# Moving the weight-split subtractions at the phase meetings from GpSimd to VectorE in a three-block transformer kernel

## The chip, the cores and the metric

One core of a Trainium2 chip runs the whole program. The metric is the device time of one execution in microseconds; a time is the median of several runs. The engines are named as the profile names them: PE is TensorE's matmuls and PEld its weight loads, DVE is VectorE, ACT is ScalarE, POOL is GpSimd, SP is SyncE, which issues most of the DMAs.

## What is computed

Three blocks follow each other on one sequence of 512 tokens, 1024 features wide, in float32. The first is gated linear attention and an MLP, the second stick-breaking attention and an MLP, the third a block that mixes an mLSTM with latent attention, and an MLP again. The reference, cut to the parts that carry the weights:

```python
def sq_relu_mlp(x, w_up, w_down):
    h = jax.nn.relu(x @ w_up)
    return (h * h) @ w_down
...
for layer in range(DEPTH):                       # two layers
    mix = gla_mixer(...) if layer < N_A else ... @ sb_w_o[j]
    h = layer_norm(DEEPNORM_ALPHA * h + mix, ln_g[layer, 0], ln_b[layer, 0])
    h = layer_norm(DEEPNORM_ALPHA * h + sq_relu_mlp(h, mlp_w_up[layer], mlp_w_down[layer]),
                   ln_g[layer, 1], ln_b[layer, 1])
...
x = x + jnp.concatenate([y_a, y_b], axis=-1) @ w_out[l]
h = rms_norm(x, g_ffn_norm[l])
x = x + jnp.square(jax.nn.relu(h @ w_ff1[l])) @ w_ff2[l]
```

## The kernel before

Activations lie feature-major: 128 partitions, eight chunks of features, 512 tokens. Every float32 matmul is done as three matmuls in the fp32r format, on a high and a low half of each operand (`mm3`, L273): the high half is the value cast to fp32r, the low half is what the cast lost. `H` and `L` are the two halves of the activations between phases, `ah` and `al` those of the hidden layer of an MLP or of an attention's output, `wh` and `wl` those of a weight tile.

Weights come as a stream of tiles of 1024 x 256 (`run`, from L1666: the list `order`). Each tile is fetched by SP in two pieces `raw`, each 128 x 1024 elements, four such buffers in all. `_split` (L196) makes the two halves of each piece: ScalarE casts `raw` to `wh` (L222), and another engine subtracts, `wl = raw - wh` (L224). A tile has two pieces, so four instructions. `q` counts quarters of a tile: the first piece is `q` 0 and 1, the second `q` 2 and 3. Tiles of the `up` matrices in the middle of an MLP go another way (`_combine`, L229), always on VectorE.

The phases meet in `boundary` (L589). It runs the last jobs of one phase (an output or down projection) on the two halves of the tokens, A and B, one after the other; behind each half the norm over it is started, in steps that are let in between the matmuls of the next jobs; then the first jobs of the next phase run on A and on B. A norm goes: residual sums into `Z` (L450, or L688), sums over pairs of chunks into `acc` (L458), their `fold` (L462), a matmul `st` with a constant matrix that spreads the mean (L473), subtraction of the mean (L516), squares `pt` on ScalarE (L478), again `acc`, `fold` and `st`, scaling (L523), gain and bias (L527), and the split into `H` (ScalarE, L503) and `L` (L505; the first two pairs of chunks on GpSimd, the last two on VectorE). `z_from_h` (L438) then forms `Z` from `H + L` (L444), half of it on GpSimd. The norm before the third block also scales `Z` on GpSimd (L548).

The order of PE's instructions is written by hand there (`manual_schedule`, L592). The orders of VectorE, ScalarE, GpSimd and SP are made by a scheduler at build time; each engine then works through its own queue strictly in that order. GpSimd's queue also holds some small DMAs (`small_load`, L142), among them the weights `wuq` and `wuk` of the latent attention.

Where `eased` (L1684) names the tile's range in the stream, the subtraction for the second piece of the tile goes to GpSimd (L223). There are five ranges, around the meetings: output projection and first `up` tiles in either layer, last `down` tiles and what follows them, and output projection and first tiles of the last MLP.

Of the kernel before, what the change touches and what calls it, by code (L numbers as in the profile page):

```python
# [10 lines left out]
F32 = mybir.dt.float32  # L11
# [3 lines left out]
ALU = mybir.AluOpType  # L15
# [48 lines left out]
class Weights:  # L64
# [5 lines left out]
    def at(self, k, cols):  # L70
        return tuple(x[:, k % self.nk, cols] for x in self.parts[k // self.nk])
# [21 lines left out]
class Model:  # L93
# [65 lines left out]
        return hi, lo  # L159


    def stream(self, order, fast, home, later, eased):


        self.order, self.fast, self.home, self.later, self.eased = order, fast, home, later, eased
        self.raws, self.ws, self.done = {}, {}, {}
        self.pos = 0

# [27 lines left out]
    def _split(self, i, n=4):  # L196

        if i >= len(self.order) or i < self.pos or i in self.later and len(self.slots) == 1:
            return
        if i in self.fast:  # L200
            if i not in self.ws:
                self._dma(i)
                self.ws[i], self.done[i] = {}, self._combine(i)
            for _ in range(1 if n < 4 else 3):
                next(self.done[i], None)
            return
        nc = self.nc
        if i not in self.ws:
            self._dma(i)
            self.ws[i], self.done[i] = Weights([], 4), 0  # L210
        parts, w, q = self.ws[i].parts, self.order[i][2], self.done[i]
        self.done[i] = min(4, q + n)
        while q < self.done[i]:

            g = q // 2
            if g == len(parts):
                parts.append(self.half_tile(i, g))
            hi, lo = parts[g]
            e = min(self.done[i], g * 2 + 2)
            a = slice(q % 2 * 2, q % 2 * 2 + (e - q) * 2)  # L220
            r = self.raws[i][g][:, a, :w]
            nc.scalar.copy(hi[:, a, :w], r)  # L222
            eng = nc.gpsimd if q >= 2 and any(p0 <= i < p1 for p0, p1 in self.eased) else nc.vector  # L223
            eng.tensor_tensor(lo[:, a, :w], r, hi[:, a, :w].bitcast(F32), op=ALU.subtract)  # L224
            q = e
        if q == 4:
            self.raws.pop(i, None)
# [1436 lines left out]
    def run(self):  # L1664
        nc = self.nc
        n4 = lambda n: [(n, i, 256) for i in range(4)]  # L1666
        mlp = lambda u, d: [(x, q * 4 + i, 256) for q in range(4) for x in (u, d) for i in range(4)]
        order = n4("gla_v")
        for hp in range(2):
            order += [("gla_q", hp, 256), ("gla_k", hp, 256), ("gla_g", hp * 2, 256), ("gla_g", hp * 2 + 1, 256)]  # L1670
        order += n4("gla_o") + mlp("up0", "down0") + n4("sb_v")
        order += [("sb_qk", i, 256) for i in range(8)]
        order += n4("sb_o") + mlp("up1", "down1")
        order += [("w2_q", 0, 256), ("w2_k", 0, 256), ("w2_cq", 0, 256), ("w2_ck", 0, 208)]
        order += [("w2_v", 0, 256), ("w2_o", 0, 256), ("w2_v", 1, 256), ("w2_o", 1, 256)]
        order += [("w2_out", 2, 256), ("w2_out", 3, 256)]
        order += [("w2_out", 0, 256), ("w2_out", 1, 256)] + mlp("ff1", "ff2")
        at = lambda n, i: next(j for j, o in enumerate(order) if o[:2] == (n, i))

        fast = {at(n, i) for n in ("up0", "up1", "ff1") for i in range(4, 16 if n == "ff1" else 15)}  # L1680
        home = {at(*x) for n in ("down0", "down1", "ff2") for x in ((n, 0), (n, 12))}
        home |= {at(*x) for x in (("gla_o", 0), ("sb_o", 0), ("w2_out", 0), ("sb_qk", 0), ("w2_v", 0))}

        eased = [(at(*a), at(*b) + 3) for a, b in (  # L1684
            (("gla_o", 1), ("up0", 3)), (("down0", 13), ("sb_v", 3)), (("sb_o", 1), ("up1", 3)),
            (("down1", 13), ("w2_ck", 0)), (("w2_out", 0), ("ff1", 3)))]
        later = {at(n, i) for n in ("gla_o", "sb_o") for i in (2, 3)}
        self.stream(order, fast, home, later, eased)
        self.setup()

        V, C = {}, {}
        for l in range(2):
            A, acc, acc2 = [], {}, {}
            out = self.out_jobs("gla_o" if l == 0 else "sb_o", A, acc)
            if l == 0:
                self.gla(A, out)
            else:
                self.sb(V, A, out)
                self.exp_tables()
            self.open_z()  # L1700
            self.open_edge()
            self.z_from_h()
            acc.update({0: self.new_acc(), 256: self.new_acc()})
            mlp = self.mlp_jobs(f"up{l}", f"down{l}", acc2)
            self.boundary(out, lambda seg: self.layer_norm(2 * l, acc[seg.start], seg), mlp[0][0])
            self.z_from_h()
            self.es.close()
            self.middle(mlp, self.Z, 1)
            self.open_edge()
            acc2.update({0: self.new_acc(), 256: self.new_acc()})  # L1710
            if l == 0:
                self.boundary(mlp[3][1], lambda seg: self.layer_norm(1, acc2[seg.start], seg), self.sb_v_jobs(V))
            else:
                def norm(seg):
                    yield from self.layer_norm_rms(3, acc2[seg.start], seg, C)
                self.xs = nc.dram_tensor("x_mid", (P, KC, S), F32).ap()
                self.boundary(mlp[3][1], norm, self.mix_first_jobs(C))
            self.es.close()
            self.zs.close()
        A = [None] * 8  # L1720
        out = self.out2_jobs(A)
        self.mix2(C, A, out[0])
        self.open_edge()
        mlp = self.mlp_jobs("ff1", "ff2", None, resid=False, final=self.out)

        def norm(seg):
            acc = self.new_acc()
            for p in range(4):
                self.square_sum(acc, p, self.zp(p, seg))
            yield from self.rms_norm("g_ffn", seg, acc, 1)  # L1730
        self.boundary(out, norm, mlp[0][0])
        self.es.close()
        self.middle(mlp, None, 0)
        self.run_jobs(mlp[3][1][:3])
        for seg in (A_, B_):
            mlp[3][1][3](seg)
        self.es.close()
        self.zs.close()
# [109 lines left out]
```

## Time and profile before

| | us |
|---|---|
| median of 3 runs | 1824.34 |
| lowest, highest | 1823.04, 1825.54 |
| the profiled execution | 1826.51 |
| its span, first to last instruction | 1824.6 |
| PE busy | 1765.2 |
| DVE busy | 1175.0 |
| ACT busy | 973.8 |
| POOL busy | 276.5 |

The busy times are of the profiled execution. Rows of the timeline give the start of an instruction in us from the first one, its duration in us, the engine, the line of the kernel, the operation, what it writes and reads, shapes, a count where equal rows follow each other, and in brackets how long the engine had stood before it and what ended that. The granted clock is given as a share of full speed.

### The profile page before, as it was taken

How to read it: one execution, taken by the hardware profiler on the slowest of the kernel's cores; microseconds unless marked ns; L12 is line 12 of the kernel's file. 1: busy time of each engine (PE TensorE's matmuls, PEld its weight loads, DVE VectorE, ACT ScalarE, POOL GpSimd, SP SyncE). 2: the span in 40 equal slices, each digit the busy share in tenths (PEclk: the TensorE clock that was granted, in tenths of full speed). 3: DMA queues.
4: the chain of work that ended last, by engine and by line, in shares of the span. 5: the costliest groups of instructions: out<-in, count | busy, mean ns of one | idle time of the engine just before them, and what ended most of it. 6: DMA issues, size and time to landing. Idle time of an engine off the chain costs nothing. (4 is left out here: it accounts for less than half of the span.)

```text
span 1824.6 us, 29591 instructions
## 1 busy us (share of the span) xinstructions
PE 1765.2 (97%) x11816; PEld 1606.5 (88%) x11816; DVE 1175.0 (64%) x1774; ACT 973.8 (53%) x1942; POOL 276.5 (15%) x315
## 2 busy tenths in 40 slices
PE   8999999999999999989999999988999999999999
PEld 8889998989899978878989898988887798989897
DVE  4545667656557388878567565483886867756562
ACT  5445464627264378764626354454777654545370
POOL 1001330000013233353300000153001321000000
PEclk9999999999999999999999999999999999999999
DMA  5212322324233111113224142332102222233231
GB/s 197 93 47 70 116 72 91 105 81 137 71 127 106 47 58 59 47 46 117 70 70 138 59 139 70 105 111 85 48 15 93 66 74 93 93 106 102 94 116 47
DMA packets 47626, 158.79 MB, mean 87 GB/s; under 512 B 5168, under 2 KB 8896, under 8 KB 47488
## 3 DMA queue, kind: packets, MB, share of 16 engines
q1 hardware_dynamic: 44752, 150.88, 25.5%
q0 software_dynamic: 1296, 3.92, 0.6%
q8 instruction: 93, 1.52, 0.3%
q10 hardware_dynamic: 1440, 2.10, 0.3%
q14 instruction: 45, 0.37, 0.1%
HBM read 152.68 MB, written 4.19 MB: 86 GB/s over the span
## 5 line engine op out<-in xcount | busy, mean ns | idle before, releaser
L275 PE MATMUL mm<-ah,wh 128*128 128x512 f32 (+1 forms) x1264 | 435.0, 344 | 3.5 <-DVE Z L1658 2.5
L276 PE MATMUL mm<-al,wh 128*128 128x512 f32 (+1 forms) x1264 | 431.8, 342 | 3.5 <-DVE al L669 2.1
L277 PE MATMUL mm<-ah,wl 128*128 128x512 f32 (+1 forms) x1264 | 430.6, 341 | 1.6 <-DVE wl L224 1.1
L224 DVE TENSOR_TENSOR wl<-raw,wh 128x1024 fp32r<-128x1024 f32 (+1 forms) x192 | 221.2, 1157 | 88.5 <-ACT wh L222 85.8
L222 ACT CAST wh<-raw 128x1024 fp32r<-128x1024 f32 (+2 forms) x238 | 223.1, 951 | 101.7 <-PE mm L276 65.0
L276 PEld LDWEIGHTS mm<-al,wh 128*128 128x128 f32 x1264 | 239.3, 189 | 34.3 <-DVE al L669 3.0
L275 PEld LDWEIGHTS mm<-ah,wh 128*128 128x128 f32 x1264 | 239.3, 189 | 33.9 <-DVE Z L1658 2.7
L277 PEld LDWEIGHTS mm<-ah,wl 128*128 128x128 f32 x1264 | 239.3, 189 | 30.9 <-DVE wl L224 1.5
L275 PE MATMUL mm<-H,wh 128*128 128x256 f32 (+1 forms) x704 | 228.9, 325 | 0.2 <-ACT sl L1198 0.2
L224 POOL TENSOR_TENSOR wl<-raw,wh 128x1024 fp32r<-128x1024 f32 (+2 forms) x46 | 118.7, 2588 | 723.4 <-ACT wh L222 681.2
L276 PE MATMUL mm<-L,wh 128*128 128x256 f32 (+1 forms) x704 | 219.8, 312 | 4.5 <-DVE L L505 4.5
L277 PE MATMUL mm<-H,wl 128*128 128x256 f32 (+1 forms) x704 | 219.6, 312 | 0.0
L275 PE MATMUL mm<-wh,H 128*128 128x256 f32 (+2 forms) x568 | 165.6, 292 | 6.9 <-ACT wh L222 6.9
L276 PE MATMUL mm<-wl,H 128*128 128x256 f32 (+2 forms) x568 | 160.9, 283 | 0.0
L277 PE MATMUL mm<-wh,L 128*128 128x256 f32 (+2 forms) x568 | 160.2, 282 | 0.0
L236 ACT CAST wh<-S 128x1024 fp32r<-128x1024 f32 x68 | 71.3, 1048 | 166.6 <-PE mm L276 152.0
L276 PEld LDWEIGHTS mm<-L,wh 128*128 128x128 f32 x704 | 134.9, 192 | 8.8 <-DVE L L505 5.3
L277 PEld LDWEIGHTS mm<-H,wl 128*128 128x128 f32 x704 | 134.2, 191 | 8.2
L275 PEld LDWEIGHTS mm<-H,wh 128*128 128x128 f32 x704 | 134.7, 191 | 6.6 <-issue 0.8
L237 DVE TENSOR_TENSOR wl<-S,wh 128x1024 fp32r<-128x1024 f32 x68 | 83.2, 1223 | 74.8 <-ACT wh L236 74.8
L688 DVE TENSOR_TENSOR Z<-Z,mm 128x512 f32<-128x512 f32 (+1 forms) x98 | 57.4, 587 | 102.7 <-PE mm L277 102.6
L275 PEld LDWEIGHTS mm<-wh,H 128*128 128x128 f32 x568 | 109.0, 192 | 8.8 <-ACT wh L222 7.6
(409 smaller groups left out, 3936.0 us busy)
## 6 DMA issues: line engine op xcount, KB each, us to landing
raw<-in_up SPq DMA_DIRECT2D x64, 512.0 KB, 4.0
raw<-in_down SPq DMA_DIRECT2D x64, 512.0 KB, 3.7
raw<-in_ff SPq DMA_DIRECT2D x64, 512.0 KB, 3.9
raw<-in_sb_qk SPq DMA_DIRECT2D x16, 512.0 KB, 3.6
raw<-in_gla_g SPq DMA_DIRECT2D x8, 512.0 KB, 4.2
raw<-in_gla_o SPq DMA_DIRECT2D x8, 512.0 KB, 3.7
raw<-in_sb_v SPq DMA_DIRECT2D x8, 512.0 KB, 4.2
raw<-in_sb_o SPq DMA_DIRECT2D x8, 512.0 KB, 3.5
```

Of the source, the lines that this page charges most:

```text
L222: nc.scalar.copy(hi[:, a, :w], r)
L224: eng.tensor_tensor(lo[:, a, :w], r, hi[:, a, :w].bitcast(F32), op=ALU.subtract)
L236: nc.scalar.copy(pair[0], t)
L237: tt(pair[1], t, pair[0].bitcast(F32), op=ALU.subtract)
L275: mm(ps, l[0], r[0], start=start, stop=False)
L276: mm(ps, l[0], r[1], start=False, stop=False)
L277: mm(ps, l[1], r[0], start=False, stop=stop)
L688: nc.vector.tensor_tensor(self.Z[:, c, seg], self.Z[:, c, seg], ps, op=ALU.add)
```

## The change

The list `eased` and the choice of engine are taken out. All subtractions of `_split` are issued on VectorE. 46 instructions are affected; their number of bytes, the casts before them, the tiles and the DMAs are the same.

```diff
-    def stream(self, order, fast, home, later, eased):
+    def stream(self, order, fast, home, later):
...
-        self.order, self.fast, self.home, self.later, self.eased = order, fast, home, later, eased
+        self.order, self.fast, self.home, self.later = order, fast, home, later
...
             nc.scalar.copy(hi[:, a, :w], r)
-            eng = nc.gpsimd if q >= 2 and any(p0 <= i < p1 for p0, p1 in self.eased) else nc.vector
-            eng.tensor_tensor(lo[:, a, :w], r, hi[:, a, :w].bitcast(F32), op=ALU.subtract)
+            nc.vector.tensor_tensor(lo[:, a, :w], r, hi[:, a, :w].bitcast(F32), op=ALU.subtract)
...
-        eased = [(at(*a), at(*b) + 3) for a, b in (
-            (("gla_o", 1), ("up0", 3)), (("down0", 13), ("sb_v", 3)), (("sb_o", 1), ("up1", 3)),
-            (("down1", 13), ("w2_ck", 0)), (("w2_out", 0), ("ff1", 3)))]
...
-        self.stream(order, fast, home, later, eased)
+        self.stream(order, fast, home, later)
```

Behind L223 of the kernel before, all lines of the changed kernel have a number smaller by one or more (L224 becomes L223, L505 becomes L504). The orders of PE and SP are the same in both builds. VectorE's order, from the last `L` of half A to the fold of half B, where the first output projection meets the first MLP; `wl18` and `wl19` are tiles of `up0`, and the middle number is the piece. Before:

```order
L505 TENSOR_TENSOR L_82<-pt_256_2337,H_81 128x2x256
L444 TENSOR_TENSOR Z_226_1955<-H_81,L_82 128x2x256
L224 TENSOR_TENSOR wl18_0_2414<-raw18_0_2409,wh18_0_2413 128x1024
L505 TENSOR_TENSOR L_82<-pt_257_2343,H_81 128x2x256
L450 SCALAR_TENSOR_TENSOR Z_226_1955<-Z_226_1955,mm_260_2421 128x256
L444 TENSOR_TENSOR Z_226_1955<-H_81,L_82 128x2x256
L224 TENSOR_TENSOR wl19_0_2481<-raw19_0_2476,wh19_0_2480 128x1024
L450 SCALAR_TENSOR_TENSOR Z_226_1955<-Z_226_1955,mm_261_2447 128x256
L458 TENSOR_TENSOR acc_233_1980<-acc_233_1980,Z_226_1955 128x512
L462 TENSOR_TENSOR fold_262_2474<-acc_233_1980 128x256
```

The two second pieces, `wl18_1` and `wl19_1`, are in GpSimd's queue here. The same stretch of VectorE's queue in the changed kernel:

```order
L504 TENSOR_TENSOR L_82<-pt_256_2337,H_81 128x2x256
L449 SCALAR_TENSOR_TENSOR Z_226_1955<-Z_226_1955,mm_260_2421 128x256
L443 TENSOR_TENSOR Z_226_1955<-H_81,L_82 128x2x256
L223 TENSOR_TENSOR wl18_0_2414<-raw18_0_2409,wh18_0_2413 128x1024
L504 TENSOR_TENSOR L_82<-pt_257_2343,H_81 128x2x256
L223 TENSOR_TENSOR wl18_1_2418<-raw18_1_2411,wh18_1_2417 128x1024
L449 SCALAR_TENSOR_TENSOR Z_226_1955<-Z_226_1955,mm_261_2447 128x256
L223 TENSOR_TENSOR wl19_0_2481<-raw19_0_2476,wh19_0_2480 128x1024
L457 TENSOR_TENSOR acc_233_1980<-acc_233_1980,Z_226_1955 128x512
L223 TENSOR_TENSOR wl19_1_2485<-raw19_1_2478,wh19_1_2484 128x1024
L461 TENSOR_TENSOR fold_262_2474<-acc_233_1980 128x256
```

Both second pieces now stand between the last `L` and the fold, one residual sum has moved ahead of the last `L`, and one `Z` has moved behind the fold.

GpSimd's queue ahead of the latent attention's first weights, with the semaphores that each row waits for. `KLp` is a tile of that attention that is set to zero, `wl101_1` the second piece of a weight tile of the third block. Before:

```order
L1427 MEMSET KLp_1609_13785 64x512 [waits PE_49,Pool_49]
L224 TENSOR_TENSOR wl101_1_13814<-raw101_1_13218,wh101_1_13813 128x512 [waits PE_49,DMAHW7_49,Activation_49,Pool_49]
L224 TENSOR_TENSOR wl101_1_13814<-raw101_1_13218,wh101_1_13813 128x512 [waits Activation_49]
L142 DMA wuq_1574_13651<-in_w_uq 128x384
L142 DMA wuk_1575_13653<-in_w_ukv 128x256
```

The two subtractions wait for the casts on ScalarE, and the DMAs behind them wait for nothing of their own. In the changed kernel:

```order
L1426 MEMSET KLp_1609_13785 64x512 [waits PE_49,Pool_49]
L142 DMA wuq_1574_13651<-in_w_uq 128x384 [waits PE_49]
L142 DMA wuk_1575_13653<-in_w_ukv 128x256
L142 DMA wuq_1625_13895<-in_w_uq 128x384
L142 DMA wuk_1626_13897<-in_w_ukv 128x256 [waits DMASW2_49]
```

The subtractions are gone from it, and the first DMA has a wait for PE instead.

VectorE's queue where the second MLP meets the third block, from the sums of squares of half A to the fold. `wl98` is a tile of the third block. Before:

```order
L458 TENSOR_TENSOR acc_1470_12782<-acc_1470_12782,pt_1473_12794 128x512
L224 TENSOR_TENSOR wl98_0_12871<-raw98_0_12866,wh98_0_12870 128x1024
L458 TENSOR_TENSOR acc_1470_12782<-acc_1470_12782,pt_1474_12799 128x512
L688 TENSOR_TENSOR Z_1178_8873<-Z_1178_8873,mm_1479_12904 128x256
L462 TENSOR_TENSOR fold_1475_12803<-acc_1470_12782 128x256
```

In the changed kernel:

```order
L457 TENSOR_TENSOR acc_1470_12782<-acc_1470_12782,pt_1473_12794 128x512
L687 TENSOR_TENSOR Z_1178_8873<-Z_1178_8873,mm_1479_12904 128x256
L457 TENSOR_TENSOR acc_1470_12782<-acc_1470_12782,pt_1474_12799 128x512
L223 TENSOR_TENSOR wl98_0_12871<-raw98_0_12866,wh98_0_12870 128x1024
L461 TENSOR_TENSOR fold_1475_12803<-acc_1470_12782 128x256
L223 TENSOR_TENSOR wl98_1_12875<-raw98_1_12868,wh98_1_12874 128x1024
```

The first piece's subtraction has moved behind the last `acc`, directly ahead of the fold, and the second piece's stands behind the fold. On ScalarE the square `pt_1474_12799` has moved ahead of the cast to `wh98_0_12870`; that is the only difference in ScalarE's order.

## Rows read from the trace of the kernel before

**Rows 1.** The page's part 1: busy us (share of the span) x instructions.
```profile
PE 1765.2 (97%) x11816; PEld 1606.5 (88%) x11816; DVE 1175.0 (64%) x1774; ACT 973.8 (53%) x1942; POOL 276.5 (15%) x315
```
**Rows 2.** PE's waits by releaser: us in total, times, longest us.
```profile
PE st L473 <- DVE fold L462: 9.5, 6, 4.7
...
PE mm L276 <- DVE L L505: 4.5, 2, 2.3
...
PE mm L276 <- DVE al L669: 2.1, 2, 1.1
...
PE pa L1563 <- DVE E L1551: 1.5, 3, 0.8
```
**Rows 3.** GpSimd's instructions on tile `wl`: ns min/median/max; idle before, us, times.
```profile
L224 POOL TENSOR_TENSOR wl<-raw,wh x46: 1267/2510/3390, 182.0 to 1519.6; 128x1024 fp32r<-128x1024 f32 x41, 128x512 fp32r<-128x512 f32 x4, 128x832 fp32r<-128x832 f32 x1
...
  ACT wh L222: 681.2, 32
```
**Rows 4.** DVE by line and form (busy us, mean ns), engines' busy us, both 300:530.
```profile
L224 DVE TENSOR_TENSOR wl<-raw,wh 128x1024 fp32r<-128x1024 f32 x20 | 24.5, 1225 | 11.6 <-ACT wh L222 11.0
...
300.00:530.00 230.00, 230.00 (x1472) 207.53 (x1471) 137.84 (x182) 110.74 (x176) 0.00 (x0) 1.00 0.30 98
```
**Rows 5.** Timelines of DVE, POOL and PE, first meeting, 228 to 240 us.
```profile
228.84 0.68 DVE L505 TENSOR_TENSOR L<-pt,H 128x512 fp32r<-128x512 f32 x1
...
231.30 2.85 DVE L505 TENSOR_TENSOR L<-pt,H 128x512 fp32r<-128x512 f32 x1
234.07 0.41 DVE L450 SCALAR_TENSOR_TENSOR Z<-Z,mm 128x256 f32<-128x256 f32 x1
...
238.43 0.69 DVE L458 TENSOR_TENSOR acc<-acc,Z 128x512 f32<-128x512 f32 x1
239.16 0.42 DVE L462 TENSOR_TENSOR fold<-acc 128x256 f32<-128x256 f32 x1
...
230.32 6.07 POOL L224 TENSOR_TENSOR wl<-raw,wh 128x1024 fp32r<-128x1024 f32 x2 [2.73 <-ACT wh L222]
...
234.20 0.38 PE L276 MATMUL mm<-L,wh 128*128 128x256 f32 x1 [2.33 <-DVE L L505]
239.64 0.70 PE L473 MATMUL st<-fold,onesd 128*128 128x256 f32 x2 [0.23 <-DVE fold L462]
```
**Rows 6.** Busy PE, PEld, DVE, ACT, POOL, then PEclk, in stretches of low clock.
```profile
234.57:237.97 3.40, 3.40 (x19) 3.40 (x18) 3.40 (x2) 1.22 (x3) 1.82 (x1) 0.50 0.46 157
...
1210.78:1217.59 6.81, 4.64 (x19) 4.46 (x20) 6.15 (x6) 2.06 (x6) 3.92 (x2) 0.50 0.97 333
1268.81:1275.62 6.81, 5.08 (x16) 4.76 (x17) 0.00 (x0) 0.79 (x4) 0.00 (x0) 0.50 0.25 97
```
**Rows 7.** Timelines of ACT, POOL, DVE and PE before the third block, 1207 to 1213.
```profile
1207.17 1.03 ACT L222 CAST wh<-raw 128x1024 fp32r<-128x1024 f32 x1
1208.57 0.63 ACT L478 ACTIVATE pt<-Z 128x512 f32<-128x512 f32 x1 [0.36 <-POOL Z L548]
...
1210.27 4.43 POOL L224 TENSOR_TENSOR wl<-raw,wh 128x1024 fp32r<-128x1024 f32 x2 [1.73 <-issue]
...
1210.46 2.44 DVE L462 TENSOR_TENSOR fold<-acc 128x256 f32<-128x256 f32 x1
...
1212.95 1.22 PE L473 MATMUL st<-fold,onesd 128*128 128x256 f32 x2 [4.75 <-DVE fold L462]
```
**Rows 8.** Timelines of PE, ACT, POOL at `wuq`, 1255 to 1271; tile `wuq`.
```profile
1255.05 0.26 PE L275 MATMUL mm<-wh,H 128*128 128x208 f32 x1
...
1264.55 0.73 ACT L1366 ACTIVATE cT<-pa,vec 128x512 f32<-128x512 f32 x1
...
1265.31 0.61 POOL L142 DMA_DIRECT2D wuq<-in_w_uq  x1
...
1270.54 1.62 PE L1391 MATMUL qp<-wuq,cT 128*128 128x192 f32 x4 [6.07 <-DMA wuq<-in_w_uq]
...
DMA to landing us min/median/max: 2.7/3.9/5.1
```

## Prediction

> **What bounds the kernel now.** I read the page's busy time first: TensorE works 1765.2 of 1824.6 us [rows 1]. So the time is its matmuls plus some 59 us in which it stands, and an edit off TensorE can only change that standing time and the clock that follows it. PE's instructions and their order are the same in both builds, so its work is taken as fixed. Next I read PE's waits by releaser [rows 2]: `st` on `fold`, 9.5 us in six waits (the longest 4.75, the row of 1212.95), matmuls on `L`, 4.5 in two, on `al`, 2.1 in two, on `E`, 1.5 in three. All four are released by VectorE, which is busy only 64% of the span, so the question is what delays VectorE at those moments.
>
> The timeline of the first meeting of phases answers it [rows 5]. `L` at L505 takes 0.68 us at 228.84. The next one, of the same shape, takes 2.85: it starts at 231.30 while GpSimd is in the first of two low-half subtractions (230.32, 6.07 us for both), and PE stands 2.33 us for it. At the place before the mixers the `fold` takes 2.44 us instead of the 0.42 of rows 5, again beside GpSimd subtractions [rows 7]. So a VectorE operation that reads two SBUF tiles is held while a GpSimd subtraction runs. `Z` from PSUM at 234.07 is not held: 0.41 us while the second one runs.
>
> The `L` and `Z` that GpSimd keeps at L505, L444 and L548 will hold VectorE as before, and I credit nothing where only they run.
>
> **What moves.** 46 subtractions leave GpSimd, 2.5 us each there [rows 3], mostly waiting for nothing but their cast on ScalarE (681.2 us of idle, which cost nothing). On VectorE the full-size one takes 1.22 us when GpSimd is idle [rows 4]. That adds at most 46 x 1.22 = 56 us to VectorE's busy time, and takes away the stretched rows. What counts is PE's waits, place by place.
>
> (a) `L` before the matmuls (2 waits, 4.5 us). In the new order the first meeting has L505 directly behind the first-half subtraction, as now, and the second-half one behind L505. Nothing holds it, so it takes 0.68: from 231.30 to 232.0, against PE's need at 234.20 - 2.33 = 231.87. Earlier stretched rows upstream shrink too, while one `Z` of 0.41 now stands ahead. I take -4.5; the bound is 0.5 left at each, -3.5.
>
> (b) `fold` outside the mixers' place (five waits, 9.5 - 4.75 = 4.75 us). Between L505 and the fold there now stand two second-half subtractions, one first-half one, one `Z` and one `acc`: 3 x 1.22 + 0.41 + 0.69 + 0.42 (the fold) = 5.2 us, so the fold ends about 236.0 if L505 ends at 230.8, 237.2 if at 232.0. PE gets there at 231.87 + (239.64 - 0.23 - 234.20) = 237.1 at the clock it had; 3.40 of those us ran at half clock [rows 6], so 235.4 without that. I leave 0.5 us of wait at this place and at its twin in the second layer, and nothing at the others: -3.75. Bounds: -4.75, and -1.15 if the fold is late by 237.2 - 235.4 = 1.8 at both.
>
> (c) `al` before the down projections (2 waits, 2.1 us). The subtraction that holds it today comes behind it in the new order: -2.1.
>
> (d) The fold before the mixers (4.75 us). PE was ready at 1212.95 - 4.75 = 1208.2 [rows 7]. The new order puts the square of the last pair ahead of the casts on ScalarE and one first-half subtraction ahead of the fold. That square starts at 1208.57, released by GpSimd's `Z` at L548, which stays. So 1208.6 + 0.63 square + 1.03 cast + 1.22 subtraction + 0.42 fold = 1211.9; less some 0.9, an estimate: upstream of this chain an `acc` is held as L505 is in rows 5, and a subtraction takes the place of the hold (2.85 - 0.68 - 1.22). That gives 1211.0. Wait 2.8 instead of 4.75: -1.95. Bounds: 0 (the chain gains nothing and the subtraction waits again) and -4.75.
>
> (e) `wuq` (6.07 us). PE stands from 1270.54 - 6.07 = 1264.47 to 1270.54 for a load that GpSimd issues at 1265.31, behind two of its subtractions, with landings of 2.7 to 5.1 us [rows 8]. Without them the four DMAs stand right behind the memset, and in the built program the first then waits for a count that PE reaches in the group just before 1255.05. Issue about 1255.2, landing by 1260.4, 4 us before PE asks. Next late is `cT`, copied from 1264.55 on (0.73), used by the `kv` matmuls behind the first `qp` ones: hidden or 0.3. I take -6.1. Bounds: 0 and -6.1. The Trainium skill, page "SBUF — State Buffer", section "Who interferes with whom", says that a DMA stalled by a VectorE operation was issued by GpSimd, which was starved of port time for writing its descriptors; with more work on VectorE this would keep the loads late, and the time would be that of rival 1. The row speaks against it so far: these four were issued while VectorE had work, and landed in 5.1 us at most.
>
> (f) `E` in the attention (1.5 us): a GpSimd subtraction lies among these steps, and the new order has it on VectorE behind the last `E` of the block. An estimate: -1.0, between 0 and the row's -1.5.
>
> (g) New cost: at gla_o the moved subtractions stand ahead of `og` and `al`. An estimate: +0.4, between 0 and one subtraction, +1.2.
>
> The sum of waits is -4.5 - 3.75 - 2.1 - 1.95 - 6.1 - 1.0 + 0.4 = -19.0 us.
>
> (h) The clock. At 234.57 the granted clock falls to 0.50 (1.2 instead of 2.4 GHz) for 3.4 us, just after the stand of 2.33 [rows 6, 5]. Three such falls, of 3.25 to 3.40 us of busy time, follow the stands at 234, 589 and 861. Two of 6.8 us follow or overlap the stands of 4.75 and 6.07. Work at half clock loses half its busy time: 3 x 3.40/2 = 5.1, 5.08/2 = 2.5, 4.64/2 = 2.3. With the stands gone I take back 5.1 and 2.5, and 0.8 of the 2.3, as a stand of 2.8 stays there: -8.4. Bounds: 0 and -9.9.
>
> Total -27.4. The profiled execution took 1826.51 us (span 1824.6), 2.2 above the median of 1824.34. Set against its own time that is 1799.1; I give it against the median: **1797**.
>
> **Rivals.**
> 1. `wuq` stays late: the descriptors are written slowly, or something else in that chain becomes late by as much. For it: the trace has only four `wuq` loads to go by. Against: 2.7 to 5.1 us to landing where 9 are to be had [rows 8]. Price 6.1 + 2.5 = 8.6: 1805.5.
> 2. The waits go, the clock falls stay (another short stand brings them): -19.0, 1805.
> 3. All of (d) goes as well: a further 2.8 + 1.5, and (b) wholly, 1.0: 1791.7.
> 4. Slower. VectorE's queue is strictly in order, so a subtraction that waits for its cast now holds what is behind it, and the long rows might be VectorE's own. At each of four meetings four second halves stand ahead of a norm's steps: 16 x 1.22 = 19.6 us more on PE's path, nothing taken away but (e): +11, 1835. It decides for slower when the stretched rows do not shrink. Against it: 1.22 and 0.68 where GpSimd is idle [rows 4, 5]. If about 22 of the 46 land whole on PE's path (22 x 1.22 = 27), the gain is just used up: no change. The Trainium skill, "Perfetto Trace Analysis", section "Optimizing Scalar/DVE Operations", allows handing work from a saturated VectorE even to GpSimd, which speaks for this rival; the same place doubts that it helps, since the two share a port, and the 2.85 beside the 0.68 agrees with the doubt.
>
> That the change does nothing is excluded: GpSimd's queue has no such row left.
>
> **How the numbers follow.** The forecast, 1793 to 1801, gets 0.60; rival 1 0.12, rival 2 0.08, rival 3 0.08, no change 0.05, rival 4 0.07. The range from 1790 to 1807 takes in the first three rivals and leaves 0.12 and some of the edges out. A measurement of this kernel can tell about 0.2%, 3.6 us, from no change. Faster 0.88, same 0.05, slower 0.07.
>
> **What would show it.** Right: in the profile after, L505, `acc` and `fold` at the meetings take 0.68, 0.69 and 0.42; PE's waits on `fold` fall to 3 to 4 us, those on `L` and `al` to nearly none; `wuq` is issued near 1255 less what was gained before, and PE's wait for it is gone; half-clock stretches are left only where the waits of the attention phases and of the last output projection stand. Wrong: long VectorE rows with GpSimd idle (rival 4), `qp` still waiting (rival 1), half-clock stretches at the same places behind short waits (rival 2).

## The result, and the profile after

The changed kernel takes **1795.84 us** (median of 4 runs, 1794.64 to 1797.53) against 1824.75 for the kernel before beside it: a ratio of 0.9836, 95% interval 0.9825 to 0.9848. That is 28.9 us less; the forecast was 27.4 less, 1797. The profiled execution took 1797.53 us, its span 1795.6.

First the busy times (engine, us, share of the span, instructions), as in [rows 1]:

```profile
PE 1756.6 (98%) x11816; PEld 1601.0 (89%) x11816; DVE 1162.6 (65%) x1820; ACT 974.9 (54%) x1942; POOL 159.0 (9%) x269
```

Then two groups of VectorE's instructions (count, busy us, mean ns of one, idle time before them):

```profile
L223 DVE TENSOR_TENSOR wl<-raw,wh 128x1024 fp32r<-128x1024 f32 x184 | 224.7, 1225 | 83.8 <-ACT wh L222 81.5
L668 DVE TENSOR_TENSOR al<-rl,ah 128x256 fp32r<-128x256 f32 x48 | 24.4, 513 | 34.6 <-ACT rl L667 34.6
```

VectorE has 46 instructions more than before and is busy 12.4 us less (1175.0 in [rows 1]). The moved ones cost 1225 ns each, as in [rows 4]; what paid for them is the rows that no longer stretch. `al` is one: 48 of them take 24.4 us, 35.5 before. PE's own work shrank by 8.6 us with the same 11816 matmuls; the other 20.4 us of the 29.0 of span are time in which PE stood. Of the 8.6, the clock explains 7.1: PE was busy for 32.9 us at half clock in the profiled execution before and for 18.7 us after, and half of each is 16.5 and 9.3. The other 1.5 us lie outside these stretches, and their cause was not found.

PE's waits (line, releaser, us in total, times, longest):

```profile
PE wt L1043 <- POOL w L1034: 7.3, 8, 3.8
PE st L472 <- DVE fold L461: 4.1, 3, 2.8
PE mm L274 <- DVE Z L1657: 2.5, 1, 2.5
PE pa L1562 <- DVE E L1550: 1.0, 2, 0.8
PE mm L275 <- DVE al L705: 1.0, 2, 0.6
```

Against [rows 2], the waits for `L` (4.5) and for `al` at L669 (2.1) have no row any more, the one for `wuq` has none, and the fold's 9.5 us in six waits are 4.1 in three. The first meeting, to be laid beside [rows 5]:

```profile
230.14 0.68 DVE L504 TENSOR_TENSOR L<-pt,H 128x512 fp32r<-128x512 f32 x1
230.74 1.21 DVE L223 TENSOR_TENSOR wl<-raw,wh 128x1024 fp32r<-128x1024 f32 x1
231.88 0.41 DVE L449 SCALAR_TENSOR_TENSOR Z<-Z,mm 128x256 f32<-128x256 f32 x1
232.21 1.21 DVE L223 TENSOR_TENSOR wl<-raw,wh 128x1024 fp32r<-128x1024 f32 x1
233.35 0.68 DVE L457 TENSOR_TENSOR acc<-acc,Z 128x512 f32<-128x512 f32 x1
233.95 1.21 DVE L223 TENSOR_TENSOR wl<-raw,wh 128x1024 fp32r<-128x1024 f32 x1
235.08 0.41 DVE L461 TENSOR_TENSOR fold<-acc 128x256 f32<-128x256 f32 x1
...
235.55 0.70 PE L472 MATMUL st<-fold,onesd 128*128 128x256 f32 x2 [0.66 <-DVE fold L461]
```

`L` takes 0.68 where its counterpart took 2.85, PE does not stand for it, and the fold behind three subtractions makes PE wait 0.66. The stretches at half clock that are left (columns: us, busy time and count by engine, granted clock, DMA share, GB/s):

```profile
776.33:783.15 6.82, 5.12 (x23) 5.11 (x24) 3.54 (x5) 3.04 (x7) 2.71 (x4) 0.50 0.23 74
1196.17:1199.58 3.41, 3.41 (x19) 3.41 (x18) 2.60 (x5) 0.09 (x1) 0.00 (x0) 0.50 0.86 302
1353.18:1356.59 3.41, 3.41 (x18) 3.31 (x17) 1.38 (x2) 1.33 (x3) 0.00 (x0) 0.50 1.00 382
1424.86:1428.27 3.41, 3.30 (x15) 3.31 (x16) 3.13 (x6) 3.41 (x5) 0.00 (x0) 0.50 0.21 52
1445.34:1448.75 3.41, 3.41 (x18) 3.41 (x17) 2.69 (x5) 2.34 (x4) 0.00 (x0) 0.50 0.00 0
```

Those behind 234, 589, 861 and 1270 us are gone, and the one before the third block is 3.41 us long instead of 6.81 [rows 6]. The one behind the longest attention wait doubled. In the kernel before it was this:

```profile
787.53:790.93 3.40, 3.34 (x16) 3.34 (x16) 0.69 (x1) 0.96 (x2) 1.09 (x3) 0.50 0.33 120
```

The doubled one begins at 776.33, while PE still stands; PE starts again only here:

```profile
778.03 1.12 PE L1043 MATMUL wt<-ident,w 128*128 128x128 f32 x4 [3.76 <-POOL w L1034]
```

So 1.7 us of it cost nothing, and PE's busy time in it is 5.12 us against 3.34.

### The profile page after: what moved, and what is told of

It is laid out like the page before. It is cut to its first block, busy times and chain, and to the rows that moved or that the text cites. A ratio compares the mean times of both kernels' runs of the same rounds, so it can differ in the third digit from the quotient of the medians.

```text
span 1795.6 us, 29581 instructions
## 1 busy us (share of the span) xinstructions
PE 1756.6 (98%) x11816; PEld 1601.0 (89%) x11816; DVE 1162.6 (65%) x1820; ACT 974.9 (54%) x1942; POOL 159.0 (9%) x269
## 4 chain that ended last, share of the span: by engine, by line
PE 81%; DVE 8%; ACT 6%; issue 3%; POOL 2%; DMA 0%; SPq 0%; DVEq 0%; ACTq 0%; POOLq 0%
PE mm L274 19%; PE mm L275 19%; PE mm L276 18%; PE a L368 11%; PE d L368 5%; PE mm L368 3%; DVE wl L223 2%; ACT wh L222 1%; DVE pr L1030 1%; PE wt L1043 1%; POOL Z L547 1%; PE pa L1562 1%; PE o L1057 0%; POOL L L504 0%; DVE wtl L1048 0%
## 5 line engine op out<-in xcount | busy, mean ns | idle before, releaser
L223 DVE TENSOR_TENSOR wl<-raw,wh 128x1024 fp32r<-128x1024 f32 (+2 forms) x238 | 265.7, 1124 | 93.1 <-ACT wh L222 90.6
L275 PEld LDWEIGHTS mm<-wl,H 128*128 128x128 f32 x568 | 108.2, 190 | 1.0
```

The lines of the kernel that those rows point to most:

```text
L223: nc.vector.tensor_tensor(lo[:, a, :w], r, hi[:, a, :w].bitcast(F32), op=ALU.subtract)
L275: mm(ps, l[0], r[1], start=False, stop=False)
```

## The experiments

Each kernel was timed beside the kernel before on the same chip (1824.22, 1824.83 and 1824.41 us in the three series). None of them leaves out any work; where work is added, it goes into a scratch tile that nothing reads.

### The `wuq` part alone, and everything but it

`e1_wuq_only` is the kernel before with one range cut short, so that three of GpSimd's 46 subtractions move: those of the mixers' first tiles, which stand ahead of the `wuq` loads in GpSimd's queue.

```diff
-        eased = [(at(*a), at(*b) + 3) for a, b in (
+        eased = [(at(*a), at(*b) + (1 if b[0] == "w2_ck" else 3)) for a, b in (
```

> The kernel before, in which only the three GpSimd subtractions ahead of the wuq loads (tiles w2_v 0 and w2_o 0) go to VectorE; the other 43 stay on GpSimd. Theory of two causes (loads queued behind subtractions, and VectorE held by GpSimd): PE's wait of 6.07 us for wuq goes, and with it the low clock behind it (5.08/2 = 2.5), so 8.6 us off 1824.7: 1816. Rival, that all of the gain is VectorE being held: 1824.7, the wait is replaced by another one.

Measured: 1817.08 us, ratio 0.9960 (0.9946 to 0.9974), 7.1 less.

`e2_all_but_wuq` is the complement: those three stay on GpSimd, the other 43 move.

```diff
-        eased = [(at(*a), at(*b) + 3) for a, b in (
-            ...
+        eased = [(at("w2_v", 0), at("w2_o", 0) + 1)]
```

> The changed kernel, in which only these three subtractions go back to GpSimd. Two causes that add: 1795.8 + 8.6 = 1804.4, with the wait for wuq back at 6 us and nothing else changed. Rival, that one cause brings all: 1795.8 or, if the loads were all of it, 1824.

Measured: 1802.01 us, ratio 0.9879 (0.9864 to 0.9894), 6.2 above the changed kernel. The timeline of GpSimd in this kernel, and PE's wait behind it:

```profile
1243.81 1.27 POOL L224 TENSOR_TENSOR wl<-raw,wh 128x512 fp32r<-128x512 f32 x1 [0.61 <-ACT wh L222]
1245.02 0.61 POOL L142 DMA_DIRECT2D wuq<-in_w_uq  x1
```

```profile
PE qp L1391 <- DMA wuq<-in_w_uq: 6.1, 1, 6.1
```

The same place in the changed kernel, GpSimd and PE:

```profile
1236.19 0.61 POOL L142 DMA_DIRECT2D wuq<-in_w_uq  x1 [0.95 <-PE mm L276]
...
1245.11 0.81 PE L1390 MATMUL qp<-wuq,cT 128*128 128x192 f32 x4
1246.14 0.70 PE L1391 MATMUL kv<-wuk,cT 128*128 128x256 f32 x2 [0.22 <-ACT cT L1365]
```

With the subtractions ahead of it the load is issued at 1245.02, behind the last of them, and `qp` stands 6.1 us. Without them it is issued at 1236.19, when PE's count comes, 8.9 us before `qp` starts; the next late one is `cT`, 0.22. So this part has a cause of its own, queueing behind GpSimd's work, and comes without any change to the held VectorE rows. By the medians it is worth 7.1 us alone (interval 4.7 to 9.9) and 6.2 last. The profiled executions can be laid side by side, as all have the same matmuls in the same order: those that take 20.0 us from 1260.1 on in the kernel before take 11.7 in `e1_wuq_only`, from 1259.5 on, and 11.7 in the changed kernel, from 1240.9 on. That is 8.3 us at the place itself, close to the 8.6 expected; what the medians lack of it lies elsewhere in the kernel and is within their noise.

### Reading or writing: what of GpSimd's work holds VectorE

Both kernels are the changed one; in both, GpSimd gets something to do at the 43 other places, and VectorE still makes every low half. In `e3_dummy_sub` it repeats the subtraction. In `e4_dummy_memset` it reads one column and then writes for 1.97 us with two memsets.

```diff
...
+            if q >= 2 and any(p0 <= i < p1 for p0, p1 in self.eased):
+                nc.gpsimd.tensor_tensor(self.junk[:, a, :w], r, hi[:, a, :w].bitcast(F32), op=ALU.subtract)
```

```diff
...
+                nc.gpsimd.tensor_tensor(self.junk[:, a, :1], r[:, :, :1], hi[:, a, :1].bitcast(F32), op=ALU.subtract)
+                for _ in range(2):
+                    nc.gpsimd.memset(self.junk[:, a, :w], 0.0)
```

> The changed kernel; at the 43 other places GpSimd in addition does the same subtraction once more, from raw and wh into a scratch tile that nobody reads. VectorE, ScalarE, SP and PE have exactly the changed kernel's order. If GpSimd's reading holds VectorE: the waits of L, fold and al come back (4.5 + 3.4 + 2.1 + 1.9 and the low clock of 5 to 6), and VectorE now also does the subtractions itself: 1813 to 1823. Rival, that the gain is VectorE's new order, or that wl is ready sooner: 1796, since neither is touched.

> As the kernel with the extra subtractions, but at each of the 43 places GpSimd reads one column and then fills the scratch tile twice with zeros, about 2.1 us of work that reads nothing. If it is GpSimd's reading of SBUF that holds VectorE: 1796, as the changed kernel. Rival, that any work on GpSimd at these places holds VectorE, or costs by its semaphores: near the kernel with the extra subtractions, 1810 or more.

Measured: `e3_dummy_sub` 1856.39 us, ratio 1.0183 (1.0165 to 1.0202): slower than the kernel before, and 60 us above the changed one, where 17 to 27 were expected. `e4_dummy_memset` 1795.87, ratio 0.9843 (0.9828 to 0.9858): the changed kernel's time to 0.03 us. The timeline of the first meeting in `e3_dummy_sub`, VectorE and GpSimd together, then its group of low halves, then PE's wait for the fold:

```profile
238.19 1.21 DVE L224 TENSOR_TENSOR wl<-raw,wh 128x1024 fp32r<-128x1024 f32 x1
238.36 6.04 POOL L226 TENSOR_TENSOR junk<-raw,wh 128x1024 f32<-128x1024 f32 x2 [2.78 <-ACT wh L223]
239.33 2.83 DVE L507 TENSOR_TENSOR L<-pt,H 128x512 fp32r<-128x512 f32 x1
242.08 3.39 DVE L224 TENSOR_TENSOR wl<-raw,wh 128x1024 fp32r<-128x1024 f32 x1
```

```profile
L224 DVE TENSOR_TENSOR wl<-raw,wh 128x1024 fp32r<-128x1024 f32 x184 | 284.1, 1549 | 77.0 <-ACT wh L223 74.5
```

```profile
PE st L475 <- DVE fold L464: 22.1, 10, 6.0
```

The same place in `e4_dummy_memset`:

```profile
229.19 0.68 DVE L509 TENSOR_TENSOR L<-pt,H 128x512 fp32r<-128x512 f32 x1
229.40 1.97 POOL L228 MEMSET junk<- 128x1024 f32 x2
229.80 1.21 DVE L224 TENSOR_TENSOR wl<-raw,wh 128x1024 fp32r<-128x1024 f32 x1
...
232.40 0.68 DVE L462 TENSOR_TENSOR acc<-acc,Z 128x512 f32<-128x512 f32 x1
232.61 1.97 POOL L228 MEMSET junk<- 128x1024 f32 x2
```

Beside a GpSimd subtraction `L` takes 2.83 us and the low half behind it 3.39; beside memsets 0.68 and 1.21. GpSimd is busy about as long in both (279.5 and 272.1 us). So not GpSimd's activity as such holds VectorE; its reading of SBUF does. The Trainium skill, page "SBUF — State Buffer", section "Who interferes with whom", says the same: a VectorE instruction with two SBUF inputs contends with a GpSimd instruction that reads SBUF, not with one that only writes it. The trace agrees, 2.83 and 3.39 against 0.68 and 1.21. The section adds that the order of issue decides who blocks. The row of 238.19 fits: it began before GpSimd's and took its 1.21, while GpSimd's two took 6.04, 3.02 each, where one that began with nothing ahead of it took 2.42 (at 224.00).

What I had wrong in this expectation is the size. I had counted the holds on the old victims alone. But the low halves that now stand on VectorE are themselves held (mean 1549 ns instead of 1225 over 184 rows, 59 us), and all of it stands in one queue. PE's waits grew by some 45 us and its busy time by 14.6.

### VectorE's queue by itself

`e8_double_dve` is the same kernel with the repeated subtraction on VectorE instead of GpSimd: no hold, only 43 more instructions in the queue.

```diff
...
+                nc.vector.tensor_tensor(self.junk[:, a, :w], r, hi[:, a, :w].bitcast(F32), op=ALU.subtract)
```

> The changed kernel, in which VectorE itself repeats the second-half subtraction into a scratch tile at the same 43 places where e3_dummy_sub let GpSimd repeat it. Nothing is left out; 43 x 1.22 = 53 us of VectorE time are added, and GpSimd stays idle there. It prices VectorE's queue by itself. By the rows of the changed kernel two such rows come to stand ahead of the fold at the first meeting and at its twin (wait 0.66 + 2.45 = 3.1, and a clock fall of 1.7 with it), and one or two ahead of the fold before the mixers; elsewhere VectorE has idle time: +9 to +16 us, 1805 to 1812. If VectorE's time as such is what the 60 us of e3_dummy_sub come from (its long subtraction rows added 59 us to VectorE), this gives about 1850 too. If VectorE has room for them all, 1796.

Measured: 1804.78 us, ratio 0.9892 (0.9876 to 0.9907), 8.9 above the changed kernel, at the low edge of what was expected. The group of the added rows, and PE's wait for the fold:

```profile
L226 DVE TENSOR_TENSOR junk<-raw,wh 128x1024 f32<-128x1024 f32 x40 | 48.8, 1220 | 0.0
```

```profile
PE st L475 <- DVE fold L464: 9.6, 10, 3.8
```

The fold's waits go from 4.1 to 9.6 us. The repeats come late in the queue's order (one of the two of the first meeting behind the fold), so fewer of them stand in PE's way than I had counted. This bears on the price of rival 4: a subtraction added to VectorE at these places costs 8.9 / 43 = 0.2 us on average, not 1.22. As the repeats stand later in the queue than the moved subtractions do, it is no exact price for those. The 60 us of `e3_dummy_sub` are thus not VectorE time as such. It adds 78 us to VectorE's busy time and this kernel 46; the first loses 0.8 us for each, the second 0.2. A reading that fits both, though no run separates it: long rows at the moments when PE waits for the queue cost more than time that the queue can shift behind them.

### One place undone at a time

Both are the kernel before with `eased` cut to one range: before the mixers, or the first meeting.

```diff
-        eased = [(at(*a), at(*b) + 3) for a, b in (
-            ...
+        eased = [(at("down1", 13), at("w2_ck", 0) + 1)]
```

```diff
-        eased = [(at(*a), at(*b) + 3) for a, b in (
-            ...
+        eased = [(at("gla_o", 1), at("up0", 3) + 3)]
```

> The kernel before with all GpSimd subtractions on VectorE but those between the second down projection and the mixers' first tiles, i.e. the change without its part (d). Nothing is left out. By the prediction's (d) and its share of (h), and the measured waits (4.75 against 2.81) and half-clock stretches (6.8 us against 3.4), this stands 1.9 + 1.7 = 3.6 us above the changed kernel: about 1799.4, with the fold waiting 4.75 us again. By the prediction's own numbers, 1.95 + 0.8: 1798.6. If the gain at that place came from the other places (work arriving earlier), 1795.8 and the wait stays 2.8.

> The kernel before with all GpSimd subtractions on VectorE but those of the first meeting of phases, i.e. the change with its first place undone. Nothing is left out. If PE's waits there come from the hold, L waits 2.3 us again, the fold 0.2 instead of 0.66, al 1.05, and the clock falls for 3.4 us behind it: +2.9 and +1.7, about 1800.4. If the clock fall at 234 us had another cause than that wait, 1798.7 and no half-clock stretch there. If the places depend on each other, another sum.

Measured: `e9_mixers_only` 1798.43 us, ratio 0.9857 (0.9841 to 0.9872), 2.6 above the changed kernel. `e10_first_only` 1798.79, ratio 0.9865 (0.9845 to 0.9884), 2.95 above. PE's wait for the fold in the first; then, of the second, two of PE's waits, PE's timeline before the mixers, and two windows with the granted clock (0.50 and 1.00 in the third column from the right):

```profile
PE st L473 <- DVE fold L462: 6.0, 3, 4.8
```

```profile
PE mm L276 <- DVE L L505: 2.3, 1, 2.3
PE mm L276 <- DVE al L669: 1.1, 1, 1.1
```

```profile
1198.35 0.48 PE L473 MATMUL st<-fold,onesd 128*128 128x256 f32 x1 [2.71 <-DVE fold L462]
```

```profile
1196.00:1206.00 10.00, 7.65 (x61) 7.55 (x62) 9.76 (x17) 6.54 (x12) 0.00 (x0) 1.00 0.87 308
234.95:238.35 3.40, 3.40 (x18) 3.40 (x17) 3.40 (x3) 1.22 (x3) 1.50 (x1) 0.50 0.37 140
```

The intervals of both overlap that of the changed kernel, so the times alone do not tell them apart from it; the waits do. Each place's waits come back and no other place's do, so the places are independent in their waits. Laid side by side, the matmuls before the mixers cost 3.4 us more in `e9_mixers_only` than in the changed kernel, 1.95 of them wait and 1.5 busy time, by the longer half clock there; the 2.6 in the medians is close to what the prediction's own terms give, 1.95 + 0.8. The first meeting costs 5.0 us more in `e10_first_only`, 3.0 of them wait and 2.1 busy time, with its fall at 235 us back, where 4.6 were expected.

But the whole profiled execution of `e10_first_only` is only 1.0 us longer than that of the changed kernel (spans 1796.6 and 1795.6). It has less half clock elsewhere: 17.1 us in all against 20.5, and none behind the fold of 1198.35 that waits 2.71, where the changed kernel has a fall behind 2.81. Whether that belongs to the edit, these runs do not show: the four runs of the changed kernel have mean granted clocks of 0.994, 0.996, 0.996 and 0.993, which by an estimate from these numbers means 14 to 25 us of half clock, so falls come and go between executions of one and the same program.

### Taking further work off GpSimd

What GpSimd still computes at the meetings was moved as well: the 20 subtractions of L504 (`e6_split_vec`), the 16 steps of L547 (`e11_z547_vec`), both (`e13_split_z547_vec`), and both with the 16 additions of L443 (`e12_all_vec`).

```diff
-        e = self.nc.gpsimd if p < 2 else self.nc.vector
+        e = self.nc.vector
...
-                nc.gpsimd.tensor_scalar(z[:, k], z[:, k], self.v("ln_g", c), self.v("ln_b", c), op0=ALU.mult, op1=ALU.add)
+                nc.vector.tensor_scalar(z[:, k], z[:, k], self.v("ln_g", c), self.v("ln_b", c), op0=ALU.mult, op1=ALU.add)
...
-                e = self.nc.gpsimd if seg is B_ else self.nc.vector
+                e = self.nc.vector
```

> The changed kernel, with the 20 subtractions of L504 that GpSimd still makes moved to VectorE as well. Nothing is left out. If what counts is the hold, this move is a wash at the first meeting: a 128x512 subtraction of 0.68 us is added, and the hold that its GpSimd row of 1.3 us causes (acc 1.35 instead of 0.68 at 225.59) goes, about 0.67 each. Before the mixers GpSimd's Z at L547 should come free 1.3 us earlier, and the fold wait fall from 2.81 to about 1.5. In all 1793 to 1797, against 1795.8. If instead every subtraction taken from GpSimd gains, as the 46 did (28.5 us / 46 = 0.6 us each), 20 of half the size gain some 6 us: 1790. If VectorE's queue is the bound, 20 x 0.68 = 14 us more in it cost up to 1800 and above.

> The changed kernel, with the 16 scale-and-shift steps of L547 (Z from Z, 128x256) moved from GpSimd to VectorE, so that what is left of the wait before the mixers is tried by itself. Nothing is left out. The prediction said of that place that the square on ScalarE is released by GpSimd's Z, which stays. If that is so, the chain gets shorter by the eight Z rows (8.6 us on GpSimd with one L504 among them, some 0.4 each on VectorE by its other 128x256 rows), the fold wait falls from 2.8 to between 0 and 1.4 us, and with it at most the 1.7 us of the clock fall behind it: 1791.3 to 1794.4. If the fold there is held by the subtractions ahead of it on VectorE instead, the wait stays at 2.8 or grows by the added rows: 1796 to 1798.

> e6_split_vec (1787.2 us) with the 16 steps of L547 on VectorE as well: around the meetings GpSimd then computes nothing. Nothing is left out. Its fold wait before the mixers is 1.4 us, with 3.4 us of half clock behind it. If GpSimd's Z is what is late there, both can go: 1784 to 1786. If the added 8 x 0.4 us stand ahead of the fold on VectorE with no gain, 1787 to 1790.

> e13_split_z547_vec with the 16 additions of L443 (Z from H and L, 128x512) on VectorE too. Nothing is left out. No one was seen to wait for these rows, and GpSimd makes four of them (6.9 us) where VectorE has only its own four to do: no gain is expected, 0 to +3 us against e13_split_z547_vec, by 16 x 0.68 = 11 us more on VectorE. If what counts were GpSimd's activity as such, this is faster again by 1 us or more.

| kernel | us | ratio to before, 95% | first fold wait before the mixers |
|---|---|---|---|
| changed kernel | 1795.84 | 0.9836 (0.9825 to 0.9848) | 2.81 |
| `e11_z547_vec` | 1793.09 | 0.9832 (0.9818 to 0.9847) | 1.66 |
| `e6_split_vec` | 1787.19 | 0.9793 (0.9776 to 0.9810) | 1.42 |
| `e13_split_z547_vec` | 1784.63 | 0.9786 (0.9771 to 0.9800) | none |
| `e12_all_vec` | 1787.19 | 0.9794 (0.9778 to 0.9810) | none |

`e6_split_vec` gained 8.6 us where I expected a wash, more than even the 6 us that its rival gave. A row of VectorE's timeline in the changed kernel (first) and the same one of this kernel (second) show what I had not counted:

```profile
224.54 0.69 DVE L443 TENSOR_TENSOR Z<-H,L 128x512 f32<-128x512 f32 x1 [1.42 <-POOL L L504]
```

```profile
223.77 0.69 DVE L443 TENSOR_TENSOR Z<-H,L 128x512 f32<-128x512 f32 x1
```

VectorE's own next step waits 1.42 us for the `L` that GpSimd makes in 1.31; on VectorE it takes 0.69, and `Z` follows without a wait. The fold of the first meeting then ends before PE asks. By the numbers, 10.1 us of span between the two profiled executions are 6.8 less PE busy time, of which half of 20.4 less 13.7 us of half clock makes 3.4, and some 3 us less waiting. The other 3.4 of busy time lie mostly behind the meetings (255 to 275, 868 to 892, 1220 to 1234 us), where the changed kernel's matmuls follow each other a little more slowly with no wait long enough to be listed; what slows them was not found.

The L547 steps shorten the wait before the mixers from 2.81 to 1.66 alone, and on top of L504 from 1.42 to nothing. In `e13_split_z547_vec` the row there has no wait (one of 0.30 stands at 1191.77, at the fold of the other half of the tokens):

```profile
1187.49 0.70 PE L472 MATMUL st<-fold,onesd 128*128 128x256 f32 x2
```

So the place was bound by GpSimd's part of the chain, as the prediction's (d) had said. In time, `e11_z547_vec` is not told apart from the changed kernel by its ratio, nor `e13_split_z547_vec` from `e6_split_vec`; the three with L504 on VectorE are faster than the changed kernel beyond both intervals. `e12_all_vec` brings nothing more, as expected. `e13_split_z547_vec` has the lowest median of this study, 1784.63 us.

## Why the prediction was right

Waits in us, by the prediction's steps:

| step | predicted | measured |
|---|---|---|
| (a) `L` | -4.5 | -4.5 |
| (b) fold, other places | -3.75, 0.5 left at each of two | -3.4, 0.66 and 0.65 left |
| (c) `al` at the down projections | -2.1 | -2.1 |
| (d) fold before the mixers | -1.95, 2.8 left | -1.9, 2.81 left |
| (e) `wuq` | -6.1 | -5.9, 0.22 left for `cT` |
| (f) `E` | -1.0 | -0.5 at `pa` L1562, -0.7 at `pa` L1544 |
| (g) `al` at gla_o | +0.4 | +0.2 |
| sum of waits | -19.0 | -18.8, and -1.6 in small ones |
| (h) clock | -8.4 | -7.1 by half-clock time, -8.6 of PE busy time in all |

(a), (b) and (c) rest on one reading of [rows 5], that a VectorE operation with two SBUF inputs is held while GpSimd subtracts. `e3_dummy_sub` and `e4_dummy_memset` show it, and narrow it to GpSimd's reading. `e10_first_only` shows that the waits of the first meeting belong to the subtractions there.

(d) named the chain behind the wait, a square on ScalarE that GpSimd's `Z` releases, then cast, subtraction and fold. After the change (ScalarE, VectorE and PE):

```profile
1191.25 0.63 ACT L477 ACTIVATE pt<-Z 128x512 f32<-128x512 f32 x1 [1.30 <-POOL Z L547]
...
1192.85 1.23 DVE L223 TENSOR_TENSOR wl<-raw,wh 128x1024 fp32r<-128x1024 f32 x1 [0.24 <-ACT wh L222]
1193.99 0.42 DVE L461 TENSOR_TENSOR fold<-acc 128x256 f32<-128x256 f32 x1
...
1194.47 0.48 PE L472 MATMUL st<-fold,onesd 128*128 128x256 f32 x1 [2.81 <-DVE fold L461]
```

From the square's start to the fold's end it is 3.16 us; the working had 0.63 + 1.03 + 1.22 + 0.42 = 3.3. The "some 0.9" that the working took off for a held `acc` upstream was the right thing too. The `acc` that starts this norm, before (first) and after:

```profile
1194.77 2.53 DVE L458 TENSOR_TENSOR acc<-Z 128x512 f32<-128x512 f32 x1
1179.22 0.68 DVE L457 TENSOR_TENSOR acc<-Z 128x512 f32<-128x512 f32 x1
```

The square then starts 0.41 us before PE is ready (1191.25 against 1191.66), where it started 0.37 us after: 0.8 us earlier. Taking the hold away shortens the chain, and GpSimd's `Z` keeps the rest, as `e11_z547_vec` shows from the other side.

(e) came out in mechanism and size, by `e1_wuq_only` and `e2_all_but_wuq`. With more work on VectorE the four `wuq` loads landed in 2.7 to 4.2 us, 2.7 to 5.1 before [rows 8], so nothing kept them late. The Trainium skill's sentence on starved descriptors (the section cited above), which the prediction set against this, does not reach this move: the same section says that `tensor_tensor`, the operation moved here, did not show the stall, which it puts down, as an inference, to its taking only the shared read interface.

(h) is right in mechanism, and nearly right by place. The three short falls went (-5.0, 5.1 forecast), and so did the one of `wuq` (-2.5, as forecast). The one before the mixers gave 4.65/2 - 3.41/2 = 0.6, where I had booked 0.8. Against these, the doubled fall behind the attention wait of 3.8 us cost (5.12 - 3.34)/2 = 0.9, and I had not thought of it; another 0.1 is scattered. That makes the 7.1 above. That PE's busy time fell by 8.6, so near to 8.4, is luck in part: 1.5 us outside the half-clock stretches, which the prediction put at nothing when it took PE's work as fixed, make up for what the clock did not bring. Half is also a little too much for a matmul at half clock: the 128x256 ones start 0.12 us apart just ahead of the fall at 1196.17 and 0.21 us apart in it.

The step that was too sure is "with the stands gone I take back" a given fall at a given place. The list of what would show it right had half clock left only behind the waits of the attention phases and of the last output projection, but one stretch before the mixers is left as well, which the sum had allowed for. And as mean clocks differ between runs of one program, a single profiled execution shows which stops got a fall in it, not which will.

Rival 4, the slower side, was rightly called unlikely, and its price was too high: not 1.22 us for each subtraction on VectorE but 0.2 on average for the repeats of `e8_double_dve`. Rival 3, the whole of (d), did not come with this change, and came with `e13_split_z547_vec`. The prediction credited nothing for `L` and `Z` that stay on GpSimd, which is right for this change; that they cost another 11 us there, it did not say.

## What to carry to other kernels

Before work goes to GpSimd to relieve VectorE, ask what VectorE has to do beside it: if VectorE's instructions there take two inputs from SBUF and GpSimd's read SBUF too, the helper can cost the helped engine more than it takes over (46 instructions more on VectorE made it 12.4 us less busy here), while memsets beside it cost nothing in these runs. Read a stretched row against the same shape elsewhere and look at what GpSimd reads at that moment, and look into GpSimd's queue for small loads that stand behind its arithmetic. Do not read much into one clock fall at one place: compare the mean granted clock of several runs.

## What the runs showed of the hardware

A stop of TensorE is not always followed by half clock, and not always by as much. The same 2.47 us stop at the same matmul is followed by 3.41 us at 0.50 in the changed kernel (at 1445.34, above), and by none in `e1_wuq_only`. The row of the changed kernel, then that of `e1_wuq_only` and its window:

```profile
1444.77 0.39 PE L274 MATMUL mm<-ah,wh 128*128 128x256 f32 x1 [2.47 <-DVE Z L1657]
1464.25 0.39 PE L275 MATMUL mm<-ah,wh 128*128 128x256 f32 x1 [2.47 <-DVE Z L1658]
```

```profile
1463.00:1474.00 11.00, 9.75 (x83) 9.70 (x84) 10.90 (x14) 5.52 (x8) 5.10 (x3) 1.00 0.31 99
```

PE waits 2.47 us in the window of `e1_wuq_only`, yet the granted clock is 1.00 throughout. The stop of 3.8 us behind the attention brought 3.41 us of half clock in the kernel before and in `e11_z547_vec`, 6.83 in the changed kernel and in `e13_split_z547_vec`. Nothing in these runs says which of the two it will be. These are single executions, and the runs of one program differ as much: 0.993 to 0.996 of mean clock in the changed kernel, and in `e13_split_z547_vec` 0.996 in the profiled run and 0.999 in the other three. So a difference of one or two falls between two profiles, up to 1.7 us of time each, is by itself no sign of what an edit did.

The other surprise is how dear the hold is when the held engine has the work too: 43 useless GpSimd subtractions, off every path, cost 60 us of 1796, more than the whole gain of the change.
